# Two tuned transformer blocks on one core: the loop for overflowing experts stands ahead of the experts, and the second block's first norm shares its sums among three engines

## The chip, the cores and the metric

The kernel runs on one core of one Trainium2 chip. A core has a matrix engine (PE, with its weight loads listed apart as PEld), a vector engine (DVE), an engine for functions and scaled copies (ACT), a general engine (POOL), a queue engine that issues most transfers (SP), and 16 DMA engines that move data between the device memory and the on-chip memory. Each of the five engines runs its own list of instructions in order and waits on semaphores for the others. The metric is the device time of the core in microseconds (us).

## The reference, cut to what matters

512 tokens of width 1024 pass through two blocks, all in float32. The first ends in a mixture of 32 experts, of which each token uses two; the second begins with a norm.

```python
def hier_moe(h, w_rg, b_rg, w_re, b_re, w_gate, w_up, w_down):
    ...                                     # group and expert logits
    top_val, top_idx = lax.top_k(e_in, TOP_K)
    gate = p_grp * jax.nn.softmax(top_val, axis=-1)
    ...                                     # tokens sorted by expert
    y = (jax.nn.silu(xb @ w_gate[e]) * (xb @ w_up[e])) @ w_down[e]
    return y * wt[:, None]
    ...
# first_block
    xl = xl + gt1 * (mix_l @ w_out[l])
    h2l = modulate(rms_norm(xl, g_ffn_norm[l]), sh2, sc2)
    xl = xl + gt2 * hier_moe(...)
    return rms_norm(xl, g_final)
# second_block, one layer
    h = rms_norm_2(x, pre_w)
    proj = h @ w_in
    ...                                     # delta rule, attention, gates
    y = merged @ w_out
    return x + rms_norm_2(y, post_w)
```

Two norms follow each other directly: `rms_norm` with `g_final` ends the first block and `rms_norm_2` begins the second. The kernel folds them into one factor per token, for which it needs two sums over the 1024 columns: of x squared, and of (x times g) squared.

## The kernel before

**Stages.** `front` computes the first block up to the attention; `second` adds the out-projection, the norm and the router (`route`); `phase_moe` runs the 32 experts in 16 pairs; `tail` is the second block.

**Experts.** An expert takes at most 64 tokens in one round (`s.cap`). For a pair, a one-hot matrix `P` is built on DVE from the ranks that the router gave, `ptk` and `pgt` (four small matmuls each) read token numbers and gates out of it, POOL gathers the 128 rows of the normed tokens by an indirect DMA into `xs`, DVE or ACT scales them to `xn`, PE transposes them (`px`, copied to `xT`), and then come the products with the weights: `pgu` (gate and up, 64 matmuls a pair) and `py` (down, 32). `po` scatters the result back with a one-hot matmul and DVE adds it to `x1`. The weights of a pair are 12 tiles `we` of 1 MB. They pass through a ring of 18 buffers (`RING`), filled by SP in order; a tile is issued when the pair that used its buffer is done with it. `gather` and `gates` of the first two pairs are issued in `route` already.

**Further rounds.** If an expert has more than 64 tokens, the kernel needs further rounds: `nrounds` is computed in `route`, and a loop with a dynamic count (`tc.For_i(0, n, 1)`) behind the experts runs all 16 pairs again for the remaining tokens. With these inputs no expert has more than 64 tokens, and the count is zero. The loop's body is 3820 instructions long over all engines. Before the loop every engine reads `nrounds` into a register and branches over the body, and behind it every engine waits for the counts of all other engines and of all DMA queues before it goes on.

**The order of the work.** Around these stages a `Recorder` takes the place of the engines: it records operations, plans an order with its own costs (`plan`), picks an engine where several can do the work (`copy`, `combine`), and issues all of it at `flush` (line 1105 in nearly all rows of the profile is that one issue). There are six flushes: two in `front`, one for `second`, one for the experts, two in `tail`. A table `ORDERS` has a line for each flush: the number of operations, four parameters, and a list of shifts of priorities (`moves`). Where the number of operations isn't the one in the table, the shifts are left out (line 1090). In the kernel before, the flushes have 1160, 901, 277, 2085, 2092 and 1883 operations against 1160, 901, 306, 1107, 2092 and 1883 in the table. At the end of a flush `Recorder.before` keeps until when the engines are busy, for the next plan; line 1405, behind the loop, sets it to nothing.

**The second block's first norm.** `tail_x2` has four tiles of 128 tokens (`t`). For each, ACT squares `x1` into a scratch half and sums (`ss0`), DVE multiplies the squares by `gf2` (the square of `g_final`, one product of 128x1024) and sums (`ss1`), small DVE operations put the sums together, POOL takes the power -1/2 (`rr1`), PE transposes the broadcast factor (`pr`), and ACT copies it into `R`. Two scratch halves serve four tiles. `R` and the transposed `x1` (`pxt`) are multiplied on DVE to `xtn`, which is split into two parts (`bh`, `bl`) for the matmuls `pgm` that follow. `w2h` and `w2l` are the same split of the second block's first weights, placed at the same time.

Of the kernel before, what the change touches and what calls it, by code (L numbers as in the profile page):

```python
# [6 lines left out]
F32 = mybir.dt.float32  # L7
F32R = mybir.dt.float32r
I32 = mybir.dt.int32
AF = mybir.ActivationFunctionType  # L10
OP = mybir.AluOpType
AX = mybir.AxisListType
PSUM = bass.MemoryType.PSUM
EPS = 1e-6
# [1117 lines left out]
class Norm2:  # L1132
# [46 lines left out]
    def route(self):  # L1179


        s, rp, ps = self.s, self.rp, self.ps
        nc, V = s.nc, s.nc.vector
        T = lambda n, *sh, d=F32: rp.tile([128, *sh], d, name=n)
        wide = lambda x, n: x.unsqueeze(2).to_broadcast([128, 4, n])

        def place(v, n, name):

            eq, gt, r = T("eq" + name, 4, n, n), T("gt" + name, 4, n, n), T("r" + name, 4, n)
            one, other = v.unsqueeze(3).to_broadcast([128, 4, n, n]), v.unsqueeze(2).to_broadcast([128, 4, n, n])  # L1190
            V.tensor_tensor(eq, other, one, op=OP.is_equal)
            V.tensor_tensor(gt, other, one, op=OP.is_gt)
            V.tensor_tensor(eq, eq, self.below[:, 0:n, 0:n].unsqueeze(1).to_broadcast([128, 4, n, n]), op=OP.mult)
            V.tensor_tensor(eq, eq, gt, op=OP.add)
            V.tensor_reduce(r, eq, axis=AX.X, op=OP.add)
            return r

        gl, el = self.lg[:, :, 0:4], self.lg[:, :, 4:36]
        gm, og, ge = T("gm", 4), T("og", 4, 4), T("ge", 4, 4)
        xe, ei, two, A = T("xe", 4, 4, 8), T("ei", 4, 8), T("two", 4, 8), T("A", 4, 32, d=F32R)  # L1200
        rg = place(gl, 4, "g")
        V.scalar_tensor_tensor(xe, rg.unsqueeze(3).to_broadcast([128, 4, 4, 8]), 0.0, el.rearrange("p t (g e) -> p t g e", g=4),
                               OP.is_equal, OP.mult)
        V.tensor_reduce(ei, xe.rearrange("p t g e -> p t e g"), axis=AX.X, op=OP.add)
        V.tensor_scalar(og, rg, 0.0, None, OP.is_equal)
        og = og.unsqueeze(3).to_broadcast([128, 4, 4, 8])
        grouped = lambda x: x.rearrange("p t (g e) -> p t g e", g=4)
        spread = lambda x: x.unsqueeze(2).to_broadcast([128, 4, 4, 8])
        r = place(ei, 8, "e")
        V.tensor_scalar(two, r, 2.0, None, OP.is_lt)  # L1210
        V.tensor_tensor(grouped(A), spread(two), og, op=OP.mult)
        flat = lambda x: x.rearrange("p t e -> p (t e)")
        p = ps.tile([128, 512], F32, tag="b", name="pr")
        nc.tensor.matmul(p[:, 0:128], s.umat, flat(A), start=True, stop=False)
        for n in (3, 2, 1):
            nc.tensor.matmul(p[:, 128 - 32 * n:128], s.onesr, flat(A[:, 0:n]), start=False, stop=n == 1)
        V.scalar_tensor_tensor(flat(s.rank), p[:, 0:128], 1.0, F(flat(A)), OP.add, OP.mult)
        s.got = {e0: gather(s, e0, s.rank, s.gx, ps) for e0 in (0, 2)}
        pc = ps.tile([128, 512], F32, tag="b", name="pc")
        for n in range(4):  # L1220
            nc.tensor.matmul(pc[:, 0:32], s.onesr, A[:, n], start=n == 0, stop=n == 3)
        mx, th = T("mx", 1), T("th", 512 // s.cap)
        V.tensor_reduce(mx, pc[:, 0:32], axis=AX.X, op=OP.max)
        V.tensor_scalar(th, s.iota[:, 1:1 + 512 // s.cap], float(s.cap), None, OP.mult)
        V.tensor_scalar(th, th, mx, None, OP.is_lt)
        V.tensor_reduce(mx, th, axis=AX.X, op=OP.add)
        V.tensor_copy(s.nrounds, mx)
        ex, sm, pg, v1, v2 = (T(n, 4) for n in ("ex", "sm", "pg", "v1", "v2"))
        g1, g2, gs = T("g1", 4, 8), T("g2", 4, 8), T("gs", 4, 32)
        V.tensor_reduce(gm, gl, axis=AX.X, op=OP.max)  # L1230
        V.tensor_tensor(ge, gl, wide(gm, 4), op=OP.subtract)
        nc.scalar.activation(ge, ge, AF.Exp)
        V.tensor_reduce(pg, ge, axis=AX.X, op=OP.add)
        V.reciprocal(pg, pg)
        V.tensor_reduce(v1, ei, axis=AX.X, op=OP.max)
        V.scalar_tensor_tensor(g2, r, 1.0, ei, OP.is_equal, OP.mult)
        V.tensor_reduce(v2, g2, axis=AX.X, op=OP.add)
        V.tensor_tensor(ex, v2, v1, op=OP.subtract)
        nc.scalar.activation(ex, ex, AF.Exp)
        V.tensor_scalar(sm, ex, 1.0, None, OP.add)  # L1240
        V.reciprocal(sm, sm)
        V.tensor_tensor(sm, sm, pg, op=OP.mult)
        V.tensor_tensor(ex, ex, sm, op=OP.mult)
        V.scalar_tensor_tensor(g1, r, 0.0, wide(sm, 8), OP.is_equal, OP.mult)
        V.scalar_tensor_tensor(g2, r, 1.0, wide(ex, 8), OP.is_equal, OP.mult)
        V.tensor_tensor(g1, g1, g2, op=OP.add)
        V.tensor_tensor(grouped(gs), spread(g1), og, op=OP.mult)
        V.tensor_copy(s.gg[:, :, :, 0], gs)
        V.tensor_tensor(s.gg[:, :, :, 1], gs, F(s.gg[:, :, :, 0]), op=OP.subtract)
        for e0 in (0, 2):  # L1250
            s.got[e0] += gates(s, e0, s.got[e0][0], s.gx, ps)


def gather(s, e0, rank, pool, ps, bufs=2):
# [108 lines left out]
def phase_moe(s, last):  # L1363
    tc, nc, i = s.tc, s.nc, s.i
    right = "right"

    def load(e0):
        return s.pre.pop(e0) if e0 in s.pre else prefetch(s, e0, ahead=False)

    with ExitStack() as st:  # L1370
        s.ringD = st.enter_context(tc.tile_pool(name="ringD", bufs=RING - 17, reuse_waits="tile"))
        xp = st.enter_context(tc.tile_pool(name="xm", bufs=2, side=right, reuse_waits="tile"))
        ps = st.enter_context(tc.tile_pool(name="ps_m", bufs=8, space=PSUM, reuse_waits="tile"))
        s.nc = Recorder(nc, tc)
        for x in s.ring:
            s.nc.tile(x)
        for e0 in range(0, 32, 2):
            got = s.got.pop(e0, None)
            if got is None:
                got = gather(s, e0, s.rank, s.gx, ps)  # L1380
                got += gates(s, e0, got[0], s.gx, ps)
            moe_pair(s, e0, got, xp, ps, load)
        last()
        s.nc.flush()
        s.nc = nc

    with ExitStack() as st:
        xp = st.enter_context(tc.tile_pool(name="xg", bufs=1, side=right, reuse_waits="tile"))
        ps = st.enter_context(tc.tile_pool(name="ps_g", bufs=8, space=PSUM, reuse_waits="tile"))
        wl = xp.tile([128, 512], F32, name="wl")  # L1390
        rk = xp.tile([128, 4, 32], F32, name="rk")
        nc.vector.tensor_copy(rk, s.rank)
        n = nc.values_load(s.nrounds[0:1, 0:1], min_val=0, max_val=512)
        with tc.For_i(0, n, 1):
            nc.vector.tensor_scalar(rk, rk, -float(s.cap), None, OP.add)
            for e0 in range(0, 32, 2):
                def load1(e0):
                    def ws(m, k, a):

                        nc.sync.dma_start(wl, expert_views(s, e0 + a)[m][:, k])  # L1400
                        return wl
                    return ws
                got = gather(s, e0, rk, xp, ps, 1)
                moe_pair(s, e0, got + gates(s, e0, got[0], xp, ps), xp, ps, load1, paired=False)
    Recorder.before = ({}, {})


RING = 18
# [110 lines left out]
def tail_x2(s, ps, sp, junk, room):  # L1519
# [13 lines left out]
    V.tensor_tensor(s.col2[:, 57:65], s.col2[:, 57:65], s.col2[:, 48:56], op=OP.mult)  # L1533
    s0, s1 = (sp.tile([128, 4], F32, name=n) for n in ("ss0", "ss1"))
    r0, r1 = (sp.tile([128, 4], F32, name=n) for n in ("rr0", "rr1"))
    R = room[:, 0:512]
    nc.combine(s.gf2, s.gf, s.gf, OP.mult)
    p = ps.tile([128, 512], F32, tag="b", name="pr2")
    for t in range(4):

        sq = junk[:, 1024 * (t % 2):1024 * (t % 2) + 1024]
        a, b, r = s0[:, t:t + 1], s1[:, t:t + 1], r1[:, t:t + 1]
        nc.scalar.activation(sq, s.x1[:, t], AF.Square, accum_out=a)
        V.scalar_tensor_tensor(sq, sq, 1.0, s.gf2, OP.mult, OP.mult, accum_out=b)
        V.tensor_scalar(a, a, 1.0 / 1024, EPS, OP.mult, OP.add)
        V.tensor_scalar(r, a, EPS, None, OP.mult)
        V.scalar_tensor_tensor(r, b, 1.0 / 1024, r, OP.mult, OP.add)
        nc.gpsimd.tensor_tensor(r, r, s.mhalf[:, 0:1], op=OP.pow)
        nc.tensor.transpose(p[:, 128 * t:128 * t + 128], r.to_broadcast([128, 128]), s.ident)
        copy(nc, R[:, 128 * t:128 * t + 128], p[:, 128 * t:128 * t + 128])  # L1550
    nc.gpsimd.tensor_tensor(r0, s0, s.mhalf[:, 0:4], op=OP.pow)
    for k in range(8):
        p = ps.tile([128, 512], F32, tag="b", name="pxt")
# [580 lines left out]
```

## Time and profile before

| | us |
|---|---|
| three runs | 1357.6, 1359.11, 1359.73 (median 1359.11) |
| profiled execution | 1358.54 |
| its span, first to last instruction | 1356.8 |
| around the span | 1.7 |
| PE busy | 1270.9 (94%) |
| DVE busy | 835.1 (62%) |
| ACT busy | 483.6 (36%) |
| POOL busy | 119.0 (9%) |
| moved by DMA | 301.72 MB |
| mean granted clock of PE, share of full | 0.977 |

The times below are microseconds from the start of the span. The router ends at about 327, the experts run from there to 837, the second block from 837 to the end. "Busy" of PE is modelled from pipelined matmuls, and a busy PE can still be waiting for weights. In the views, `[x <-Y]` behind an instruction is the idle time of its engine before it and what seems to have ended it. A releaser is inferred, and where an instruction waits for nothing in the code the name given there is only what happened to end last.

### The profile page before, as it was taken

How to read it: one execution, taken by the hardware profiler on the slowest of the kernel's cores; microseconds unless marked ns; L12 is line 12 of the kernel's file. 1: busy time of each engine (PE TensorE's matmuls, PEld its weight loads, DVE VectorE, ACT ScalarE, POOL GpSimd, SP SyncE). 2: the span in 40 equal slices, each digit the busy share in tenths (PEclk: the TensorE clock that was granted, in tenths of full speed). 3: DMA queues.
4: the chain of work that ended last, by engine and by line, in shares of the span. 5: the costliest groups of instructions: out<-in, count | busy, mean ns of one | idle time of the engine just before them, and what ended most of it. 6: DMA issues, size and time to landing. Idle time of an engine off the chain costs nothing. (4 is left out here: it accounts for less than half of the span.)

```text
span 1356.8 us, 18378 instructions
## 1 busy us (share of the span) xinstructions
PE 1270.9 (94%) x7123; PEld 824.1 (61%) x7123; DVE 835.1 (62%) x1649; ACT 483.6 (36%) x992; POOL 119.0 (9%) x121
## 2 busy tenths in 40 slices
PE   5999998998999999998999996799999999999998
PEld 3778676777445444343434433578777777777786
DVE  5788899857235444444344435778544886567774
ACT  5655375312223112111110101367553775346521
POOL 1223320011000000000000001201000100000010
PEclk9999999998999999999999998799999999999999
DMA  9975320159899999999999981322111221322231
GB/s 342 325 268 178 129 79 14 49 225 413 347 420 420 420 417 419 419 420 420 419 420 419 420 316 31 124 74 83 50 47 64 63 63 63 93 63 70 99 127 62
DMA packets 94229, 301.72 MB, mean 222 GB/s; under 512 B 9915, under 2 KB 43812, under 8 KB 69558
## 3 DMA queue, kind: packets, MB, share of 16 engines
q1 hardware_dynamic: 90166, 287.87, 55.1%
q0 software_dynamic: 3392, 10.50, 2.1%
q10 hardware_dynamic: 576, 2.10, 0.4%
q8 instruction: 58, 0.95, 0.3%
q14 instruction: 37, 0.30, 0.1%
HBM read 294.14 MB, written 6.31 MB: 221 GB/s over the span
## 5 line engine op out<-in xcount | busy, mean ns | idle before, releaser
L1105 PE MATMUL pgu<-we,xT 128*64 128x512 f32 x1024 | 272.0, 600 | 0.0
L1105 PEld LDWEIGHTS pgu<-we,xT 128*64 128x64 f32 x1024 | 88.1, 138 | 138.7 <-issue 130.6
L1105 DVE TENSOR_TENSOR x<-x,po 128x512 f32<-128x512 f32 x152 | 97.2, 682 | 73.8 <-PE po L1105 73.6
L1105 PE MATMUL py<-we,hT 128*64 128x512 f32 x512 | 137.3, 604 | 3.9 <-DVE hT L1105 2.8
L1105 PE MATMUL pgm<-bl,w2h 128*128 128x512 f32 x352 | 136.2, 406 | 0.0
L1105 PE MATMUL pgm<-bh,w2h 128*128 128x512 f32 x352 | 135.7, 405 | 0.0
L1105 PE MATMUL pgm<-bh,w2l 128*128 128x512 f32 x352 | 134.7, 405 | 0.4 <-DVE w2l L1105 0.4
L1105 ACT ACTIVATE hs<-pgu 128x512 f32<-128x512 f32 x16 | 9.6, 598 | 339.3 <-PE pgu L1105 339.3
L1105 DVE SCALAR_TENSOR_TENSOR yt<-py,gs,gt 128x512 f32<-128x512 f32 x32 | 24.0, 751 | 131.4 <-PE py L1105 121.1
L1105 PEld LDWEIGHTS py<-we,hT 128*64 128x64 f32 x512 | 47.5, 138 | 66.0 <-issue 58.6
L1105 PEld LDWEIGHTS pgm<-bh,w2l 128*128 128x128 f32 x352 | 66.0, 189 | 15.2 <-issue 1.2
L1105 PEld LDWEIGHTS pgm<-bl,w2h 128*128 128x128 f32 x352 | 66.3, 189 | 14.3 <-issue 1.4
L1105 PEld LDWEIGHTS pgm<-bh,w2h 128*128 128x128 f32 x352 | 66.3, 189 | 13.8 <-issue 0.3
L1105 DVE TENSOR_TENSOR w2l<-w,w2h 128x2048 fp32r<-128x2048 f32 (+1 forms) x26 | 54.2, 2086 | 5.6 <-ACT w2h L1105 5.1
L1105 PE MATMUL po<-yh,PT 128*128 128x512 f32 x128 | 44.0, 434 | 13.2 <-DVE yh L1105 13.0
L1105 POOL DMA_INDIRECT xs<-xnd,idx x16 | 17.0, 1062 | 396.8 <-DVE idx L1105 149.6
L1105 ACT ACTIVATE xT<-px,mod 128x128 f32<-128x128 f32 x74 | 27.9, 458 | 63.4 <-PE px L1105 54.3
L1105 PEld LDWEIGHTS po<-yh,PT 128*128 128x128 f32 x128 | 23.3, 192 | 38.4 <-issue 15.1
L1105 DVE TENSOR_TENSOR hs<-hs,pgu 128x512 f32<-128x512 f32 x16 | 10.9, 684 | 56.1 <-ACT hs L1105 56.1
L1105 PE MATMUL po<-yl,PT 128*128 128x512 f32 x128 | 43.0, 424 | 2.2 <-DVE yl L1105 2.2
L1105 ACT ACTIVATE ada<-ada,sc 128x256 f32<-128x256 f32 x69 | 29.8, 501 | 17.0 <-DMA ada<-in_w_ada_dram 17.0
L1105 PEld LDWEIGHTS po<-yl,PT 128*128 128x128 f32 x128 | 24.1, 195 | 16.4 <-DVE yl L1105 6.8
(568 smaller groups left out, 2624.8 us busy)
## 6 DMA issues: line engine op xcount, KB each, us to landing
we<-in_w_gate_dram SPq DMA_DIRECT2D x64, 1024.0 KB
we<-in_w_up_dram SPq DMA_DIRECT2D x64, 1024.0 KB
we<-in_w_down_dram SPq DMA_DIRECT2D x64, 1024.0 KB
ada<-in_w_ada_dram SPq DMA_DIRECT2D x24, 1024.0 KB
w<-in_w_in_dram SPq DMA_DIRECT2D x24, 1024.0 KB
win<-in_w_in_dram SPq DMA_DIRECT2D x8, 1024.0 KB
wout<-in_w_out_dram SPq DMA_DIRECT2D x4, 1024.0 KB
wo<-in_w_out_dram SPq DMA_DIRECT2D x4, 1024.0 KB
```

What stands on the lines that cost most here:

```text
L1105: x = op.alts[e][0](*op.args, **op.kw)
```

## The change

The loop for further rounds moves from behind the experts to ahead of them, between the router and the experts, and is wrapped in a condition `tc.If(n > 0, ...)` whose false side falls through. The reset of `Recorder.before` behind the loop goes. The gather and the gates of the second pair leave `route` and are recorded with the experts, behind the loop. With this, the loop's wait for all engines and queues behind the body isn't passed when the count is zero; what an engine runs then is the reading of `nrounds`, the branch, a wait for its own count (SP: for all its transfers to have landed; POOL: for all of its own), and a branch over the body.

In `tail_x2`, the sum of (x times g) squared is made in two ways: for the first two token tiles POOL multiplies `x1` by `g_final` and ACT squares and sums; for the other two DVE does it as before. The four factors go into one tile `pr`, copied once. A few small operations are joined. The first flush of the second block has 2088 operations instead of 2092, `second` has 262 instead of 277, the experts 2100 instead of 2085; the other flushes keep their numbers.

```diff
@@ route
-        s.got = {e0: gather(s, e0, s.rank, s.gx, ps) for e0 in (0, 2)}
+        s.got = {0: gather(s, 0, s.rank, s.gx, ps)}
...
-        for e0 in (0, 2):
-            s.got[e0] += gates(s, e0, s.got[e0][0], s.gx, ps)
+        s.got[0] += gates(s, 0, s.got[0][0], s.gx, ps)
@@ phase_moe
+    with ExitStack() as st:
...
+        nc.vector.tensor_copy(rk, s.rank)
+        n = nc.values_load(s.nrounds[0:1, 0:1], min_val=0, max_val=512)
+        with tc.If(n > 0, preferred_fallthrough_block=False), tc.For_i(0, n, 1):
+            nc.vector.tensor_scalar(rk, rk, -float(s.cap), None, OP.add)
...
     with ExitStack() as st:
         s.ringD = st.enter_context(tc.tile_pool(name="ringD", bufs=RING - 17, reuse_waits="tile"))
...
-        n = nc.values_load(s.nrounds[0:1, 0:1], min_val=0, max_val=512)
-        with tc.For_i(0, n, 1):
...
-    Recorder.before = ({}, {})
@@ tail_x2
-    R = room[:, 0:512]
+    half = lambda x, n: x[:, 1024 * n:1024 * n + 1024]
+    pr = ps.tile([128, 512], F32, tag="b", name="pr2")
+    R = s.nat[1].rearrange("p c h d -> p (c h d)")[:, 0:512]
     nc.combine(s.gf2, s.gf, s.gf, OP.mult)
-    p = ps.tile([128, 512], F32, tag="b", name="pr2")
     for t in range(4):
-        sq = junk[:, 1024 * (t % 2):1024 * (t % 2) + 1024]
         a, b, r = s0[:, t:t + 1], s1[:, t:t + 1], r1[:, t:t + 1]
+        sq = half(junk, t % 2)
         nc.scalar.activation(sq, s.x1[:, t], AF.Square, accum_out=a)
-        V.scalar_tensor_tensor(sq, sq, 1.0, s.gf2, OP.mult, OP.mult, accum_out=b)
-        V.tensor_scalar(a, a, 1.0 / 1024, EPS, OP.mult, OP.add)
-        V.tensor_scalar(r, a, EPS, None, OP.mult)
+        if t < 2:
+            xg = half(room, t)
+            nc.gpsimd.tensor_tensor(xg, s.x1[:, t], s.gf, op=OP.mult)
+            nc.scalar.activation(xg, xg, AF.Square, accum_out=b)
+        else:
+            V.scalar_tensor_tensor(sq, sq, 1.0, s.gf2, OP.mult, OP.mult, accum_out=b)
+        V.tensor_scalar(r, a, EPS / 1024, EPS * EPS, OP.mult, OP.add)
         V.scalar_tensor_tensor(r, b, 1.0 / 1024, r, OP.mult, OP.add)
         nc.gpsimd.tensor_tensor(r, r, s.mhalf[:, 0:1], op=OP.pow)
-        nc.tensor.transpose(p[:, 128 * t:128 * t + 128], r.to_broadcast([128, 128]), s.ident)
-        copy(nc, R[:, 128 * t:128 * t + 128], p[:, 128 * t:128 * t + 128])
+        nc.tensor.transpose(pr[:, 128 * t:128 * t + 128], r.to_broadcast([128, 128]), s.ident)
+    copy(nc, R, pr)
+    V.tensor_scalar(s0, s0, 1.0 / 1024, EPS, OP.mult, OP.add)
     nc.gpsimd.tensor_tensor(r0, s0, s.mhalf[:, 0:4], op=OP.pow)
```

PE between the router and the first expert product, before. `warm` are matmuls whose result nobody reads:

```order
1067 L1105 MATMUL pgt<-gg,P 128x4 x8
1068 L1105 MATMUL ptk<-tokid,P 128x4 x4
1069 L1105 MATMUL pgt<-gg,P 128x4
1070 L1105 MATMUL ptk<-tokid,P 128x4 x4
1071 L1105 MATMUL pgt<-gg,P 128x4 x7
1072 L1105 MATMUL ptk<-tokid,P 128x4 x8
1073 L1105 MATMUL pgt<-gg,P 128x4 x4
1074 L1105 MATMUL px<-ident,xn 128x128 x8
1075 L1105 MATMUL pgu<-we_00_2699,xT 64x512
```

The same on PE with the change; the rows left out in the middle are the loop's body:

```order
1065 L1105 MATMUL pgt<-gg,P 128x4 x4
1066 L1376 TENSOR_LOAD nrounds
1067 L1377 COMPARE_AND_BRANCH
1068 L1377 UNCONDITIONAL_BRANCH
...
1443 L1105 MATMUL ptk<-tokid,P 128x4 x8
1444 L1105 MATMUL pgt<-gg,P 128x4 x8
1445 L1105 MATMUL ptk<-tokid,P 128x4 x8
1446 L1105 MATMUL pgt<-gg,P 128x4 x8
1447 L1105 MATMUL ptk<-tokid,P 128x4 x4
1448 L1105 MATMUL px<-ident,xn 128x128 x8
1449 L1105 MATMUL pgu<-we_00_2699,xT 64x512
```

The branch now stands between the first pair's `pgt` and everything else, and nine groups of four small matmuls stand between it and `px`.

SP at the same place, before. `we` are expert tiles, `gt_1479` the row of gates for the add:

```order
86 L1105 DMA we_04_2713<-in_w_gate_dram 128x2048
87 L1105 DMA gt_1479<-rowd 128x1024
88 L1105 DMA we_10_3121<-in_w_up_dram 128x2048
89 L1105 DMA we_10_3122<-in_w_up_dram 128x2048
90 L1105 DMA we_04_3120<-in_w_gate_dram 128x2048
91 L1105 DMA we_14_3123<-in_w_up_dram 128x2048
```

The same on SP with the change:

```order
87 L1105 DMA gt_1479<-rowd 128x1024
88 L1376 TENSOR_LOAD nrounds
89 L1376 ISA x2
90 L1105 DMA we_10_6407<-in_w_up_dram 128x2048
91 L1377 COMPARE_AND_BRANCH
92 L1377 UNCONDITIONAL_BRANCH
...
147 L1105 DMA we_10_6408<-in_w_up_dram 128x2048
148 L1105 DMA we_04_6406<-in_w_gate_dram 128x2048
149 L1105 DMA we_14_6409<-in_w_up_dram 128x2048
```

Two of the tiles that fill the ring before the experts start now stand behind SP's branch, and at that branch SP waits for everything that it has issued to land.

POOL at the second block's first norm, before (`ogT` holds `g_final`, `rr_9249` the factors of the four token tiles, `nat` the halves that take the products):

```order
56 L1105 TENSOR_TENSOR w2l<-w_2560_0_3778,w2h 128x512
57 L1105 TENSOR_TENSOR w2l<-w_2560_4_3779,w2h 128x512 x2
58 L1105 TENSOR_TENSOR rr_9249<-rr_9249,mhalf 128x1 x2
59 L1105 TENSOR_TENSOR w2l<-w_2560_0_3778,w2h 128x512
60 L1105 TENSOR_TENSOR wabl<-sv,wabh 128x64
61 L1105 TENSOR_TENSOR rr_9248<-ss_9246,mhalf 128x4
62 L1105 TENSOR_TENSOR rr_9249<-rr_9249,mhalf 128x1 x2
```

And with the change:

```order
60 L1105 TENSOR_TENSOR ogT<-ogT 128x1024
61 L1105 TENSOR_TENSOR w2l<-w_2560_0_7064,w2h 128x512
62 L1105 TENSOR_TENSOR nat_9238<-x_1468,ogT 128x1024 x2
63 L1105 TENSOR_TENSOR rr_9250<-rr_9250,mhalf 128x1 x3
64 L1105 TENSOR_TENSOR wabl<-sv,wabh 128x64
65 L1105 TENSOR_TENSOR rr_9250<-rr_9250,mhalf 128x1
66 L1105 TENSOR_TENSOR rr_9249<-ss_9247,mhalf 128x4
```

POOL takes over the product `gf2` and two products of 128x1024 and gives up three of its four `w2l`.

## Rows read from the trace of the kernel before

**Rows 1.** The page: busy time, share of the span and instructions of each engine.

```profile
PE 1270.9 (94%) x7123; PEld 824.1 (61%) x7123; DVE 835.1 (62%) x1649; ACT 483.6 (36%) x992; POOL 119.0 (9%) x121
```

**Rows 2.** Busy time in stretches; the last three columns are PE's clock, DMA share, GB/s.

```profile
328.00:340.00 12.00, 7.21 (x32) 6.98 (x33) 6.67 (x23) 0.00 (x0) 0.57 (x1) 0.50 1.01 416
340.00:344.00 4.00, 4.00 (x14) 1.79 (x14) 2.59 (x6) 1.51 (x4) 1.35 (x2) 0.50 0.79 294
344.00:348.00 4.00, 4.00 (x18) 1.48 (x16) 0.00 (x0) 0.00 (x0) 0.07 (x1) 0.90 0.48 134
348.00:352.00 4.00, 4.00 (x21) 1.66 (x19) 0.00 (x0) 0.00 (x0) 0.00 (x0) 1.00 0.86 311
356.00:800.00 444.00, 422.60 (x1880) 187.35 (x1878) 198.41 (x376) 67.92 (x126) 12.84 (x12) 0.99 1.01 419
816.00:828.00 12.00, 10.09 (x38) 3.47 (x36) 1.72 (x2) 0.00 (x0) 0.00 (x0) 0.86 0.00 0
```

**Rows 3.** Timeline from the router to the experts: start, us, instruction [idle before, releaser].

```profile
323.19 0.43 SPq L1105 DMA_DIRECT2D we<-in_w_gate_dram  x1
...
325.01 1.17 POOL L1105 DMA_INDIRECT xs<-xnd,idx  x1 [10.48 <-DVE g L1105]
...
326.08 1.02 PE L1105 MATMUL pgt<-gg,P 128*128 128x4 f32 x8
...
333.50 0.99 PE L1105 MATMUL ptk<-tokid,P 128*128 128x4 f32 x4 [0.16 <-DVE P L1105]
...
337.28 0.16 DVE L1105 CAST idx<-ptk 128x1 int32<-128x1 f32 x1 [3.24 <-DMA xs<-xnd,idx]
...
338.02 1.14 DVE L783 TENSOR_SCALAR xn<-xs,rn 128x1024 f32<-128x1024 f32 x1
...
339.22 1.97 PE L1105 MATMUL px<-ident,xn 128*128 128x128 f32 x8 [3.88 <-DVE xn L783]
...
341.12 4.16 PE L1105 MATMUL pgu<-we,xT 128*64 128x512 f32 x10
...
347.45 0.80 SPq L1105 DMA_DIRECT2D we<-in_w_up_dram  x2
```

**Rows 4.** The 16 gathers `xs` of the experts, from issue to landing.

```profile
DMA to landing us min/median/max: 4.7/9.0/12.4
```

**Rows 5.** Timeline across the loop behind the experts.

```profile
832.75 3.75 DVE L1105 TENSOR_TENSOR x<-x,po 128x512 f32<-128x512 f32 x6
...
836.55 0.42 DVE L1105 CAST w2h<-w 128x512 fp32r<-128x512 f32 x1
...
837.36 1.06 ACT L1105 ACTIVATE qT<-x 128x1024 f32<-128x1024 f32 x1 [5.67 <-DVEq L1394]
837.43 1.27 POOL L1105 TENSOR_TENSOR w2l<-w,w2h 128x512 fp32r<-128x512 f32 x1 [109.08 <-DVEq L1394]
...
839.69 4.82 PE L1105 MATMUL pxt<-ident,x 128*128 128x128 f32 x27 [5.39 <-DMA sv<-in_a_log_dram]
...
841.33 1.39 DVE L1105 CAST w2h<-w 128x512 fp32r<-128x512 f32 x1 [4.36 <-DMA caus<-in_k_mask_dram]
```

**Rows 6.** Timeline of the second block's first norm.

```profile
846.38 1.21 DVE L1105 TENSOR_TENSOR ogT<-ogT 128x1024 f32<-128x1024 f32 x1
...
847.65 1.21 DVE L1105 SCALAR_TENSOR_TENSOR qT<-qT,ogT 128x1024 f32<-128x1024 f32 x1
...
848.90 1.06 ACT L1105 ACTIVATE qT<-x 128x1024 f32<-128x1024 f32 x1 [7.15 <-DVE qT L1105]
...
850.16 2.28 POOL L1105 TENSOR_TENSOR rr<-rr,mhalf 128x1 f32<-128x1 f32 x2 [4.92 <-DVE col L1105]
...
852.42 1.94 POOL L1105 TENSOR_TENSOR w2l<-w,w2h 128x512 fp32r<-128x512 f32 x1
...
858.03 0.27 ACT L1105 COPY nat<-pr 128x128 f32<-128x128 f32 x1 [0.56 <-PE pr L1105]
858.33 1.41 DVE L1105 SCALAR_TENSOR_TENSOR xtn<-pxt,col,nat 128x512 f32<-128x512 f32 x2 [3.89 <-ACT nat L1105]
```

**Rows 7.** The second block's first flush: busy time of the stretch, columns as in rows 2.

```profile
862.00:1075.00 213.00, 211.91 (x2186) 165.44 (x2186) 138.71 (x282) 121.46 (x285) 14.00 (x16) 1.00 0.21 70
```

**Rows 8.** Who waited for whom in that stretch: total us, times, longest.

```profile
PEld pY L1105 <- issue: 4.2, 12, 0.4
...
PEld pZ L1105 <- issue: 3.8, 11, 0.4
```

More of the change, by code (lines that the diff above doesn't have):

```diff
@@ L1370, in phase_moe, with load1, ws @@
     with ExitStack() as st:
+        xp = st.enter_context(tc.tile_pool(name="xg", bufs=1, side=right, reuse_waits="tile"))
+        ps = st.enter_context(tc.tile_pool(name="ps_g", bufs=8, space=PSUM, reuse_waits="tile"))
+        wl = xp.tile([128, 512], F32, name="wl")
+        rk = xp.tile([128, 4, 32], F32, name="rk")
+        nc.vector.tensor_copy(rk, s.rank)
+        n = nc.values_load(s.nrounds[0:1, 0:1], min_val=0, max_val=512)
+        with tc.If(n > 0, preferred_fallthrough_block=False), tc.For_i(0, n, 1):
+            nc.vector.tensor_scalar(rk, rk, -float(s.cap), None, OP.add)
+            for e0 in range(0, 32, 2):
+                def load1(e0):
+                    def ws(m, k, a):
+                        nc.sync.dma_start(wl, expert_views(s, e0 + a)[m][:, k])
+                        return wl
+                    return ws
+                got = gather(s, e0, rk, xp, ps, 1)
+                moe_pair(s, e0, got + gates(s, e0, got[0], xp, ps), xp, ps, load1, paired=False)
+    with ExitStack() as st:
         s.ringD = st.enter_context(tc.tile_pool(name="ringD", bufs=RING - 17, reuse_waits="tile"))
@@ L1385, in phase_moe @@
         s.nc = nc
[L1387 to L1392, printed above, removed]
-        n = nc.values_load(s.nrounds[0:1, 0:1], min_val=0, max_val=512)
-        with tc.For_i(0, n, 1):
[L1395 to L1404, printed above, removed]
-    Recorder.before = ({}, {})
 RING = 18
```

## The prediction

> **What bounds the kernel now.** I read the page first: PE is busy 94% of the span [rows 1], so the kernel looks bound by PE. The table of stretches says that this is not one limit. From 356 to 800 the DMA share is 1.01 at 419 GB/s [rows 2]: the experts are bound by their weights, and PE's high busy share there is a model's overlap. Whatever delays the stream of weights before that stretch is paid in full behind it, since no later part of the stream has room to catch up. From 862 to 1075 PE is busy 211.91 of 213.00 us [rows 7]: the second block is bound by PE. The two seams between these stages are where nothing is full. From 816 to 828 no transfer runs [rows 2], and from 834.30 to the first `xtn` at 858.33 PE has only transposes [rows 5, 6]. [...] The change takes work from the second seam and puts some into the first. I read both in the timeline, and in the order which instructions go where.
>
> **The seam behind the experts.** The last add to `x1` ends at 832.75+3.75 = 836.50 [rows 5]. ACT and POOL, which had branched long before, go on at 837.36 and 837.43. DVE and PE had to finish first: DVE's cast ends at 836.97 and its next one, which waits for nothing in the code, starts 4.36 us later at 841.33; PE ends at 834.30 and its next starts 5.39 us later [rows 5]. So reading the count and branching over 3820 instructions costs the engine that comes last 4.4 to 5.4 us, when the DMA engines are idle. With the change this is gone here: the norm begins at 836.5, PE's transposes run right behind `po`, and the plan of the second block starts from the engines' state at the experts' end.
>
> Then the chain of the norm. Before: the squares of the third tile wait until 848.90 for a scratch half, 7.15 us, because DVE makes `gf2` at 846.38 and the first weighted sum at 847.65 only [rows 6]; then powers, two groups of transposes with four copies, and `xtn` at 858.33. After, from 836.5: ACT has six squares of 1.06 instead of four, none waiting for a half to be freed by DVE. POOL makes `gf2` before the end of the experts, then two products of 128x1024. The trace shows no such product on POOL; its 128x512 product took 1.27 us [rows 5] and 1.94 beside DVE [rows 6], so twice that, 2.5 to 3.9 us each. I take 2.5, because DVE has fewer weighted sums to run beside it: 836.5+5.1 = 841.6. The second square ends at 842.7, small operations 0.4, two powers at 1.14 each (2.28 for two [rows 6]) 845.4. Transposes and the copy: one copy in place of four, between 0.27 (one of before) and 1.08 (four), say 0.6; with 0.5 for the last transpose 846.5. DVE meanwhile has two weighted sums and seven splits of `w2`, some 9 us in all, which is the other leg and ends near 848 to 849. I take `xtn` at 849.0 against 858.33: a gain of 9.3 us. Bounds: 6, if each POOL product takes 3.9; 11, if DVE's leg is no longer than POOL's. The branch is 4.4 of it, the chain the rest.
>
> [...]
>
> **The seam ahead of the experts.** PE ends the first pair's `pgt`, half of the eight that took 1.02 [rows 3], by 327.1 at the latest and branches. I call J the time from there to its next matmul. Nine groups of four `ptk` or `pgt` follow in the new order, each about 0.99 at half clock [rows 3]: 8.9 us, with DVE's `P`, casts and reductions between. Before, seven groups (28 matmuls) stood in the same place, and DVE waited 3.24 us for a gather anyway, until 337.28 [rows 3]; this wait goes, since the second gather now stands behind the branch. Then `xn` (1.14, started 1.20 before `px`) and 1.90 from `px` to `pgu` [rows 3]. The first `pgu` comes at 327.1+J+8.9+1.2+1.9 = 339.1+J, against 341.12. J is not shown at this place. From below it is 0, if the branch is hidden as it was for ACT: `pgu` 2.0 earlier. The branch behind the experts gives 5.4: 3.4 later. [...] I take J = 6.5, nearest to the row of the same branch with a little for the load: `pgu` at 345.6, 4.5 us later.
>
> [...]
>
> SP waits at its branch until all it issued has landed, and two tiles that were issued by 323.6 [rows 3] stand behind. With 2 MB less queued the stream runs dry 5 us before 340, at 335; SP goes on 4.4 to 5.4 later, at 340, and sends 2 MB, 5 us. The stream was to pause for the ring anyway: after these two tiles all depends on the first `pgu` again, 6.33 us before the next issue [rows 3]. So SP's hole lies inside the ring's and costs nothing by itself, and the stream restarts as much later as `pgu` does. As the stretch to 800 is full, the 4.5 us arrive at its end.
>
> **The lost shifts.** The second block's first flush had its 26 shifts of priorities, since 2092 operations stood in the table; with 2088 it has none. The PE work is the same. Its chain of small products `pY` and `pZ` waits 4.2 and 3.8 us now [rows 8]. If the unshifted order covered them half as well, +8; an order without shifts may also be as good, or better by a part of the 1.1 us that PE idles, -1. As the order still has large `pgm` and `psv` between these products, I take +2. The other flushes keep their tables' state, and the first two of them their order.
>
> **Sum.** Against the profiled execution, 1358.54 (0.57 under the median of the runs, 1359.11): 1358.54 - 9.3 + 4.5 + 2 = 1355.7. It takes about 0.2%, 2.7 us, to tell a difference from none here: 1356.4 to 1361.8 is "the same".
>
> **The rivals.**
> *The branch is hidden.* J = 0, `pgu` 2.0 earlier: 1358.54 - 9.3 - 2.0 + 2 = 1349.2. For it speaks ACT, which branched early and resumed at once; against it DVE and PE, which waited 4.4 and 5.4 with nothing to wait for. Chance 0.14.
> *The branch is dear in the loaded stretch; slower than before.* The place is between `pgt` and the next `ptk` on PE. [...] It decides from J = 9.4, where the sum is 1358.5. [...] Chance 0.25.
> *The unshifted order costs what it can.* +8 in place of +2: 1361.7. For it: a long serial chain; against: 1.1 us of idle PE in 213. Chance 0.15.
> *The shared norm does nothing.* If POOL's products at 3.9 and its powers form a chain as long as DVE's was, only the branch's 4.4 remains of the gain: 1360.6, the same as before. Chance 0.10.
>
> **How the numbers follow.** My forecast, 0.36, holds 1352 to 1360 by J from 5 to 8, a gain of 8 to 11 and 0 to 4 for the order; two thirds of it lie under 1356.4. With the first rival and the good ends of the others, faster has 0.44. The rest of the forecast, the fourth rival and half of the third are the same: 0.27. Slower is the dear branch and what it adds to the third: 0.29. The range reaches from the hidden branch to two fetches, 1347 to 1367.
>
> **What would show it.** Right: behind the experts no pause of 4 us on DVE and PE, `xtn` 12 to 13 us behind the last add to `x1` instead of 22, the first `pgu` near 345.6, the time at which the DMA share falls at the end of the experts moved by the same 4 to 5, and the stretch from the first `pgm` to the end of the first flush longer by at most 4. Wrong: PE's pause behind the first `pgt` under 2 or over 9 us; an end of the experts that doesn't follow the first `pgu`; a POOL product of 128x1024 over 4 us on the way to `xtn`; new idle PE before `pY` and `pZ`.

## The result and the profile after

The changed kernel takes 1373.47 us in the median of four runs (1372.02 to 1374.86), before 1358.45: it is 1.06% slower, ratio 1.0106 with a 95% interval of 1.0092 to 1.0120. The forecast was 1355.7, with 1347 to 1367 as the range. The profiled execution took 1372.02, its span 1369.9.

The page's first part answers to [rows 1]; PE has the same 7123 instructions and is busy 7.9 us longer:

```profile
PE 1278.8 (93%) x7123; PEld 830.3 (61%) x7123; DVE 835.0 (61%) x1649; ACT 487.4 (36%) x988; POOL 120.2 (9%) x121
```

I cut both spans at the same events and subtract. Each time is the start of a row of the timelines; the last column is what the prediction had.

| stretch | before | after | change | predicted | 
|---|---|---|---|---|
| start to the first `pgu` | 341.12 | 345.72 | +4.6 | +4.5 |
| first `pgu` to the last pair's `hp` | 475.6 | 479.0 | +3.5 | 0 |
| last `hp` to the end of the last add to `x1` | 19.8 | 22.6 | +2.8 | 0 |
| last add to the first `xtn` | 21.8 | 12.1 | -9.7 | -9.3 |
| first `xtn` to the first `z` | 212.8 | 224.7 | +11.9 | +2 |
| first `z` to the end | 285.7 | 285.7 | 0 | 0 |
| span | 1356.8 | 1369.9 | +13.1 | -2.8 |

(`hp` is the product of the two halves of a pair on DVE, once a pair; the first `z` is the first score of the second block's attention, behind the first flush.) Two terms came out as predicted. Two that I had at nothing cost 6.3 us, and one that I had at 2 cost 11.9.

One trace stands behind each column, and single traces scatter. Four kernels have the orders of before up to the end of the experts (before itself and, below, the runs without shifts, with the norm alone and without the loop): in their traces the last add ends between 831.3 and 837.4, and the stretch from the first `pgu` to the last `hp` takes 473.5 to 476.7. A difference of 3 us in a stretch of the experts is therefore hardly clear of the scatter, and the two middle rows need the experiments.

**The router and the experts' start**, timeline of the kernel after, columns as in [rows 3]:

```profile
326.03 0.58 PE L1105 MATMUL pgt<-gg,P 128*128 128x4 f32 x4
326.28 16.22 SPq L1105 DMA_DIRECT2D we<-in_w_up_dram  x2
...
333.18 1.83 PE L1105 MATMUL ptk<-tokid,P 128*128 128x4 f32 x8 [6.58 <-issue]
...
342.56 1.14 DVE L783 TENSOR_SCALAR xn<-xs,rn 128x1024 f32<-128x1024 f32 x1 [0.22 <-issue]
...
343.85 1.94 PE L1105 MATMUL px<-ident,xn 128*128 128x128 f32 x8 [1.70 <-DVE xn L783]
...
345.72 15.83 PE L1105 MATMUL pgu<-we,xT 128*64 128x512 f32 x64
352.08 0.80 SPq L1105 DMA_DIRECT2D we<-in_w_up_dram  x2
```

PE stops for 6.58 us at the branch. SP's first tile behind its branch is the second of the merged 326.28 row. The next ring-limited issue is at 352.08, 6.36 behind `pgu`, as it was 6.33 behind before. At the other end of the stream the DMA share (second last column) falls some 4 to 5 us later, as the prediction had it; before, then after:

```profile
798.00:802.00 4.00, 3.77 (x17) 1.36 (x18) 2.33 (x4) 0.62 (x1) 0.00 (x0) 1.00 0.68 281
```

```profile
798.00:802.00 4.00, 4.00 (x22) 1.59 (x18) 0.00 (x0) 0.00 (x0) 0.00 (x0) 1.00 1.01 420
802.00:806.00 4.00, 3.49 (x15) 1.18 (x11) 1.39 (x3) 0.00 (x0) 0.00 (x0) 1.00 0.81 336
```

**The 13th pair.** DVE's `hp` of the 12th and 13th pair, each with PE's last large group of `pgu` of the 13th pair; first before, then after with two more rows of what lies between:

```profile
693.72 1.05 DVE L1105 TENSOR_TENSOR hp<-hs,pgu 128x512 f32<-128x512 f32 x1
...
721.04 3.65 PE L1105 MATMUL pgu<-we,xT 128*64 128x512 f32 x14
...
724.73 1.05 DVE L1105 TENSOR_TENSOR hp<-hs,pgu 128x512 f32<-128x512 f32 x1 [1.53 <-PE pgu L1105]
```

```profile
699.17 1.05 DVE L1105 TENSOR_TENSOR hp<-hs,pgu 128x512 f32<-128x512 f32 x1
...
729.21 1.14 DVE L783 TENSOR_SCALAR xn<-xs,rn 128x1024 f32<-128x1024 f32 x1
730.41 0.66 PE L1105 MATMUL px<-ident,xn 128*128 128x128 f32 x4 [1.72 <-DVE xn L783]
730.99 3.65 PE L1105 MATMUL pgu<-we,xT 128*64 128x512 f32 x14
...
734.68 1.05 DVE L1105 TENSOR_TENSOR hp<-hs,pgu 128x512 f32<-128x512 f32 x1 [4.10 <-PE pgu L1105]
```

31.0 us between them before, 35.5 after. In the new order PE makes the transposes `px` of later pairs ahead of this pair's last `pgu`, and waits for their `xn`. The pairs behind it take 30 to 31 us in both kernels, so most of the step stays. As the stream of weights falls off only 4 to 5 us later, this part of the delay isn't the stream's.

**The seam behind the experts.** Before, the last `yh` and `yl` on DVE:

```profile
828.89 0.43 DVE L1105 CAST yh<-yt 128x512 fp32r<-128x512 f32 x1
829.35 0.69 DVE L1105 TENSOR_TENSOR yl<-yt,yh 128x512 fp32r<-128x512 f32 x1
```

After, the same and the norm behind it, answering to [rows 5, 6]:

```profile
836.57 1.89 POOL L1105 TENSOR_TENSOR ogT<-ogT 128x1024 f32<-128x1024 f32 x1 [131.23 <-DMA sv<-in_w_in_dram]
...
836.93 1.82 DVE L1105 CAST yh<-yt 128x512 fp32r<-128x512 f32 x1
...
838.78 1.65 DVE L1105 TENSOR_TENSOR yl<-yt,yh 128x512 fp32r<-128x512 f32 x1
...
844.88 2.48 DVE L1105 TENSOR_TENSOR x<-x,po 128x512 f32<-128x512 f32 x4 [0.68 <-PE po L1105]
...
845.72 5.16 POOL L1105 TENSOR_TENSOR nat<-x,ogT 128x1024 f32<-128x1024 f32 x2 [5.84 <-DVE x L1105]
...
848.64 2.26 DVE L1105 TENSOR_TENSOR col<-col 128x8 f32<-128x8 f32 x1
...
858.87 0.59 ACT L1105 COPY nat<-pr 128x512 f32<-128x512 f32 x1 [5.16 <-PE pr L1105]
859.49 1.41 DVE L1105 SCALAR_TENSOR_TENSOR xtn<-pxt,col,nat 128x512 f32<-128x512 f32 x2 [2.09 <-ACT nat L1105]
```

The pauses of 4.36 and 5.39 us of [rows 5] are gone. But POOL now makes `gf2`, and a `w2l` right behind it, while DVE is in the last pair's results, and DVE's cast takes 1.82 us instead of 0.43, `yl` 1.65 instead of 0.69. From the start of the `yt` ahead of this cast to the end of the last add it is 11.2 us, 8.4 before.

**The second block's first flush**, `xtn` to `z`: busy time of the stretch, columns as in [rows 2]; before with one piece of it, then after with three, answering to [rows 7]:

```profile
858.00:1071.00 213.00, 211.22 (x2175) 163.49 (x2175) 139.14 (x279) 119.37 (x276) 12.92 (x15) 0.99 0.23 77
...
922.00:932.00 10.00, 10.00 (x58) 8.36 (x57) 7.64 (x18) 7.42 (x15) 0.00 (x0) 1.00 0.31 105
```

```profile
859.00:1084.00 225.00, 219.95 (x2175) 168.01 (x2175) 140.43 (x284) 118.88 (x270) 13.62 (x18) 0.96 0.21 71
...
916.00:922.00 6.00, 5.21 (x29) 3.92 (x27) 6.00 (x9) 4.75 (x10) 0.00 (x0) 1.00 0.07 6
922.00:932.00 10.00, 9.42 (x35) 7.51 (x35) 6.41 (x19) 3.65 (x9) 2.64 (x1) 0.54 0.60 206
932.00:938.00 6.00, 5.57 (x25) 4.08 (x24) 2.34 (x11) 3.05 (x9) 3.15 (x2) 0.91 0.00 0
```

The same 2175 PE instructions take 225 us instead of 213. PE idles 5.05 us (225 - 219.95) instead of 1.78. The granted clock is 0.96 in the mean instead of 0.99. As an estimate, a microsecond at a granted clock c loses 1-c of its work (before, four `ptk` take 0.50 us at a clock of 1.00, at 324.02, and 1.01 at 0.50, at 328.46); from the means that is 9.0 us lost instead of 2.1, each uncertain by 1 for the rounding. From the pieces it is less: from 922 to 938 5.1 us are lost (0.46 of 10 and 0.09 of 6) where nothing was lost before. So idle time and clock make 8 to 10 of the 12 us, and the rest stays open. From 922 to 932 the clock is 0.54: 0.72 in the first 2 us and 0.50 in the 8 behind them. What PE did before it fell:

```profile
917.74 1.05 PE L1105 MATMUL psq<-ones,sq 128*128 128x1 f32 x8
...
919.57 1.05 PE L1105 MATMUL psq<-ones,sq 128*128 128x1 f32 x8 [0.78 <-ACT sq L1105]
...
922.63 1.67 PE L1105 MATMUL psq<-ones,sq 128*128 128x1 f32 x8 [0.55 <-ACT sq L1105]
```

Groups of matmuls one column wide, close together, with waits for ACT ahead of them (0.78 and 0.55 us); the third already takes 1.67 us instead of 1.05. Before, the same groups come 4 to 5 us apart, with no wait, and `pgm` fills the time between them:

```profile
917.87 0.39 PE L1105 MATMUL pgm<-bh,w2l 128*128 128x512 f32 x1
918.09 0.95 PE L1105 MATMUL psq<-ones,sq 128*128 128x1 f32 x8
...
922.23 0.95 PE L1105 MATMUL psq<-ones,sq 128*128 128x1 f32 x8
```

Who waited for whom in the stretch after, answering to [rows 8]; in the stretch before no wait at `psq` is listed:

```profile
PEld pY L1105 <- issue: 5.5, 15, 0.7
...
PEld pZ L1105 <- issue: 4.1, 12, 0.4
...
PE psq L1105 <- ACT sq L1105: 1.3, 2, 0.8
```

### The profile page after: what moved, and what is told of

The parts are those of the page before. It is cut to its first block, busy times and chain, and to the rows that moved or that the text cites. A ratio compares the mean times of both kernels' runs of the same rounds, so it can differ in the third digit from the quotient of the medians.

```text
span 1369.9 us, 18350 instructions
## 1 busy us (share of the span) xinstructions
PE 1278.8 (93%) x7123; PEld 830.3 (61%) x7123; DVE 835.0 (61%) x1649; ACT 487.4 (36%) x988; POOL 120.2 (9%) x121
## 4 chain that ended last, share of the span: by engine, by line
PE 61%; issue 7%; DVE 5%; ACT 1%; POOL 1%; DVEq 0%; POOLq 0%; ACTq 0%
PE pgu L1105 16%; PE pgm L1105 14%; PE py L1105 12%; PE po L1105 5%; PE pbr L1105 3%; PE psv L1105 2%; PE C L1105 2%; PE pso L1105 1%; PE px L1105 1%; DVE yt L1105 1%; PE pZ L1105 1%; PE pY L1105 1%; DVE hp L1105 1%; DVE yl L1105 1%; PE ph L1105 1%
## 5 line engine op out<-in xcount | busy, mean ns | idle before, releaser
L1105 PE MATMUL pgu<-we,xT 128*64 128x512 f32 x1024 | 276.2, 604 | 0.0
L1105 PE MATMUL py<-we,hT 128*64 128x512 f32 x512 | 142.0, 604 | 4.6 <-DVE hT L1105 3.2
L1105 PE MATMUL pgm<-bh,w2h 128*128 128x512 f32 x352 | 129.5, 410 | 0.0
L1105 PE MATMUL pgm<-bl,w2h 128*128 128x512 f32 x352 | 129.1, 407 | 0.0
L1105 PE MATMUL pgm<-bh,w2l 128*128 128x512 f32 x352 | 128.7, 408 | 0.4 <-DVE w2l L1105 0.4
L1105 PEld LDWEIGHTS pgm<-bh,w2h 128*128 128x128 f32 x352 | 65.7, 191 | 13.1 <-issue 0.3
L1105 ACT CAST w2h<-w 128x2048 fp32r<-128x2048 f32 (+1 forms) x23 | 33.1, 1458 | 15.6 <-PE pgm L1105 8.2
```

What stands on the lines that cost most here:

```text
L1105: x = op.alts[e][0](*op.args, **op.kw)
```

## The experiments

Each ratio is to runs of the kernel before on the same chip in the same session (medians there 1356.95 to 1358.04). With the 1358.45 above, the medians of the kernel before differ by up to 1.5 us, so two experiments are best compared by their ratios. Three things had to be told apart: the lost shifts, the moved loop, and the shared norm.

**The shifts left out of the kernel before.**

```diff
-    (2092, 0.0, 1, 0, 400, (
+    (0, 0.0, 1, 0, 400, (
```

> The kernel before with one number of the table changed, so that the second block's first flush gets no shifts; all else as before. Theory (the lost shifts cost the 12 us that the changed kernel is slower between its first xtn and the first z): about 1358.5 + 12 = 1370 us, and a stretch of about 5 to 10 us between 900 and 940 in which PE's granted clock is at half. Rival (the flush is slow because of what stands ahead of it, the new norm and the later start; the shifts are worth 4 us at most): 1358 to 1362 us, PE's clock at full from 865 on.

Measured: 1375.85 us, ratio 1.0152 (1.0122 to 1.0182). One number of a table, with not an operation changed, costs 19 us. The stretch:

```profile
858.00:1087.00 229.00, 222.07 (x2178) 168.27 (x2178) 140.78 (x288) 118.74 (x268) 12.99 (x17) 0.97 0.20 66
```

16 us longer than before, with 6.9 us of idle PE and, as expected, a piece at half clock (0.50 from 922 to 928). The loss is larger than the 12 expected; idle and clock account for some 10 of the 16, the rest lies between matmuls that the profile counts as busy and stays open. PE waits for `sq` at `psq` here too (0.9 us in two waits, the longer 0.8), as in the changed kernel. The rival is out.

**The loop moved alone** (the norm of before, so 2092 operations and the shifts).

```diff
 def tail_x2(s, ps, sp, junk, room):
-    ... (the changed kernel's)
+    ... (before's)
```

> The changed kernel with the norm of before: only the loop is moved. 2092 operations, so the shifts are in force; PE's order from the first pab to the first z is that of before. Theory: start +4.6 us at the first pgu, the experts' end some 4 to 8 later than before, the branch behind them gone (4.4 less), the flush as long as before: 1358.5 + 4.6 + 3.5 - 4.4 = 1362 us, between 1358 and 1364. Rival (what stands ahead of the flush makes it slow): 1370 us or more.

Measured: 1358.93 us, 1.0016 (1.0005 to 1.0028). The flush takes 212.4 us, 212.8 before. So moving the loop is a small loss: first `pgu` at 345.02, experts' end 9.6 us later (846.10 against 836.50), `xtn` 2.2 earlier. POOL's collision with DVE is here too, with the norm of before, since there too the plan gives `gf2` to POOL (`combine` lets it choose):

```profile
835.31 1.89 POOL L1105 TENSOR_TENSOR ogT<-ogT 128x1024 f32<-128x1024 f32 x1 [131.46 <-DMA sv<-in_w_in_dram]
...
835.40 2.08 DVE L1105 CAST yh<-yt 128x512 fp32r<-128x512 f32 x1
...
837.52 1.65 DVE L1105 TENSOR_TENSOR yl<-yt,yh 128x512 fp32r<-128x512 f32 x1
```

From the last add to `xtn` it is 10.0 us, less than the 12.1 of the changed kernel with its shared norm. The time is in the range of the theory; the rival is out.

**The norm alone** (the loop behind the experts, 2088 operations, no shifts).

```diff
 def tail_x2(s, ps, sp, junk, room):
-    ... (before's)
+    ... (the changed kernel's)
```

> The kernel before with the changed norm alone; the loop stays behind the experts, 2088 operations, no shifts. Theory: the norm's chain is some 4 to 5 us shorter, the lost shifts cost 12: 1358.5 - 4.5 + 12 = 1366 us. Rival: 1354 to 1358 us.

Measured: 1371.89 us, 1.0115 (1.0093 to 1.0138). Later than the 1366 expected, because the shifts cost more than 12 on this side: the flush takes 232.9 us, and the clock falls a second time in it (0.79 from 980 to 1000, 0.87 from 1000 to 1020). The rival is out. In the first experiment, which lacks the shifts too, the median is 4 us longer, but the two intervals overlap, and the traces don't give this gain to the norm. The chain from the last add to `xtn` is 4.0 us shorter here (17.1 against 21.1), the flush 4.6 longer (232.9 against 228.3), and the last add ends 4.0 earlier (833.45 against 837.40), ahead of anything that the norm could change.

**The changed kernel with the shifts in force.**

```diff
     nc.gpsimd.tensor_tensor(r0, s0, s.mhalf[:, 0:4], op=OP.pow)
+    idle = sp.tile([128, 4], F32, name="idle")
+    for t in range(4):
+        V.memset(idle[:, t:t + 1], 0.0)
```

> The changed kernel with four tiny memsets of an unread tile in the norm, so that the flush has 2092 operations and the shifts hit the same operations as before; PE's order from the first pab to the first z is nearly that of before. Theory: 1373.5 - 12 = 1361.5 us. Rival (the shifts aren't it): 1371 to 1374 us.

Measured: 1362.15 us, 1.0040 (1.0028 to 1.0052), against 1.0106 without the four instructions: 0.66 of the 1.06% are back, 9 us by the ratios and 11.3 by the medians. The rival is out. The stretch takes 212.5 us from `xtn` to `z`, against 224.7; its clock is at 0.99, and the waits at `pY` and `pZ` are again 4.2 and 3.8, those of [rows 8]:

```profile
862.00:1075.00 213.00, 211.48 (x2177) 163.61 (x2178) 139.40 (x279) 119.74 (x277) 13.75 (x17) 0.99 0.24 79
```

**gf2 on ACT**, and **the second pair's gather back in the router**, each on the loop moved alone, then both.

```diff
-    nc.combine(s.gf2, s.gf, s.gf, OP.mult)
+    nc.scalar.activation(s.gf2, s.gf, AF.Square)
```

> The loop moved alone (norm of before, shifts in force), and the product gf2 made by ACT as a square instead of by POOL; no other operation changes its number. In the loop-alone run POOL makes gf2 from 835.31 to 837.20 and w2l right behind, and DVE's cast yh, which takes 0.43 us before, takes 2.08, its yl 1.65 instead of 0.69. Theory (POOL's products hold up DVE at the end of the experts): both go back to about 0.4 and 0.7, the last add to x1 comes 2 to 3 us sooner behind the last py, and the run is 2 to 3 us shorter than loop alone (1358.9): 1356 to 1357. Rival (DVE is slow there for another reason): cast and yl as in loop alone, time the same as loop alone.

Measured: 1356.26 us, 0.9984 (0.9975 to 0.9993), 0.32% under the loop alone (1.0016). The rival is out: DVE's operations are short again, and from the start of the `yt` ahead of the cast to the end of the last add it is 8.1 us:

```profile
838.14 0.43 DVE L1105 CAST yh<-yt 128x512 fp32r<-128x512 f32 x1
838.60 0.69 DVE L1105 TENSOR_TENSOR yl<-yt,yh 128x512 fp32r<-128x512 f32 x1
```

```diff
-        s.got = {0: gather(s, 0, s.rank, s.gx, ps)}
+        s.got = {e0: gather(s, e0, s.rank, s.gx, ps) for e0 in (0, 2)}
...
-        s.got[0] += gates(s, 0, s.got[0][0], s.gx, ps)
+        for e0 in (0, 2):
+            s.got[e0] += gates(s, e0, s.got[e0][0], s.gx, ps)
```

> The loop moved alone, but the gather and gates of the second pair stay in the router as before; the experts' flush has 2085 operations again and its PE order in the last pairs is that of before. Theory (the experts end late for two reasons: 4.5 us at the first pgu, and 4 us at the 13th pair, where the new order has px ahead of the pair's last pgu): first pgu at 343 to 344, the step of 35.5 us between the 12th and 13th hp back at about 31, experts' end 2 to 4 us later than before instead of 9.6 (of which 2.6 is POOL against DVE, which stays), time 1352 to 1355 us. Rival (the lag at the 13th pair comes from the later start and the stream of weights): the step stays near 35, and only the 1 to 2 us at the first pgu are gained: 1357 to 1358 us.

Measured: 1353.06 us, 0.9967 (0.9957 to 0.9978). The 13th pair is back at 31.0 us:

```profile
698.52 1.05 DVE L1105 TENSOR_TENSOR hp<-hs,pgu 128x512 f32<-128x512 f32 x1
...
729.54 1.04 DVE L1105 TENSOR_TENSOR hp<-hs,pgu 128x512 f32<-128x512 f32 x1 [1.53 <-PE pgu L1105]
```

So the late start isn't what delays it, but the order, which the planner made from 2100 operations instead of 2085. All traces bear this out: the step is 31.0 to 32.8 us in the eight kernels whose experts' flush has 2085 operations and 35.5 to 37.2 in the four that have 2100, and the stretch from the first `pgu` to the last `hp` is 473.5 to 477.1 in the eight and 478.3 to 481.4 in the four. The expected gain at the first `pgu` was a miss: it came at 346.56, not at 343 to 344. The experts end at 839.40, 2.9 us later than before, which is within the scatter of single traces.

> Both edits on the loop moved alone: gf2 on ACT, and the second pair's gather in the router. If both theories hold their gains add: 1350 to 1353 us. If neither does, 1358 to 1359 us as loop alone.

Measured: 1352.0 us, 0.9955 (0.9941 to 0.9969). The gains don't add in full: with the gather in the router the plan had moved POOL's product off DVE's way already. From the last but one `yt` to the end of the last add it took 8.2 us there, against 11.5 in loop alone, and POOL's product ran beside six adds that didn't become longer (3.75 us for six, as in [rows 5]):

```profile
835.06 2.43 POOL L1105 TENSOR_TENSOR ogT<-ogT 128x1024 f32<-128x1024 f32 x1 [13.22 <-DMA sv<-in_g_final_dram]
...
835.65 3.75 DVE L1105 TENSOR_TENSOR x<-x,po 128x512 f32<-128x512 f32 x6
```

**No loop**, with the orders of before: rounds beyond the first are left out, and nothing else.

```diff
-        with tc.For_i(0, n, 1):
-            ...
```

> The kernel before without the loop for further rounds (left out: rounds beyond the first, which these inputs don't need); the reset of the planner's state stays, so all orders are those of before. Theory (the branch behind the experts holds DVE 4.4 us and PE 5.4): 4 to 5 us under before, DVE's cast at 841.33 comes at 837, the norm's chain otherwise as before: about 1353 us. Rival (the pause hides behind transfers or the norm's other chain): within 1 us of before.

Measured: 1353.53 us, 0.9964 (0.9951 to 0.9977), some 5 us (0.36%) under before. The rival is out. PE goes on 1.03 us behind its last `po` and not 5.39, waiting for the add alone:

```profile
827.69 1.45 PE L1105 MATMUL po<-yl,PT 128*128 128x512 f32 x5
830.17 3.22 PE L1105 MATMUL pxt<-ident,x 128*128 128x128 f32 x27 [1.03 <-DVE x L1105]
```

**The shared norm where nothing else disturbs it**: the run with both edits, with the changed kernel's norm, `gf2` on ACT in it, and the four memsets. This is the changed kernel with three repairs.

> The loop ahead, the second pair's gather in the router, gf2 on ACT, the shifts in force by four tiny memsets, and now the shared norm (POOL multiplies x1 by g for two token tiles, one copy of the factors). So the shared norm is the one difference of weight to the run with both edits (1352.0 us). Theory (POOL's two products of 128x1024 take 2.5 us each and hold up DVE while they run, so that the shared norm is longer once nothing else delays the chain: 10.0 us from the last add to the first xtn in loop alone, 12.1 in the changed kernel): 2 to 3 us longer, 1354 to 1355 us. Rival (it was only gf2 on POOL that did harm; without it the shared norm is the shorter one): 1349 to 1351 us.

Measured: 1350.51 us, 0.9949 (0.9932 to 0.9965), the same within the intervals as without the shared norm. From the last add to `xtn` it is 11.4 us here (in the trace of an execution of 1353.74 us) and 11.3 there. The theory is out: no loss shows. The time lies in the rival's 1349 to 1351, but its reason, a shorter chain, doesn't show, and a gain of 0.06% (0.9949 against 0.9955) is far within the intervals. POOL takes 4.89 us for its two products, and DVE stands behind them: an operation on 128x8 elements takes 2.33 us beside them. In the run with both edits the first two of DVE's weighted sums take 2.16 and 2.21 us and the other two 1.21; in the run with `gf2` on ACT alone the one that runs beside a `w2l` of POOL (846.56, 1.28 us) takes 2.34 and the others 1.21 to 1.22.

**Both edits, and no loop anywhere** (rounds beyond the first left out).

```diff
-        with tc.If(n > 0, preferred_fallthrough_block=False), tc.For_i(0, n, 1):
-            ...
```

> The run with both edits, without the loop (left out: rounds beyond the first, not needed by these inputs): no branch anywhere, the planner's state carried on. The difference to the run with both edits (1352.0 us) is the price of the branch ahead of the experts. Theory (the branch stops PE for 6.6 us in the middle of a serial chain; 4 to 5 us of it arrive at the first pgu and all of these at the end): 1347 to 1348 us, first pgu at 340 to 341. Rival (the later start is made good while the experts wait for weights): 1350 to 1352 us.

Measured: 1347.58 us, 0.9922 (0.9908 to 0.9936), 4.5 us (0.33%) under the run with both edits. The first `pgu` comes 5.4 us earlier:

```profile
340.14 2.83 PE L1105 MATMUL pgu<-we,xT 128*64 128x512 f32 x6
```

The theory holds, and the rival is out. So the branch ahead of the experts costs 4.5 us at the end, the same as the branch behind them: moving it gained nothing by itself.

A gain of another kind shows against the run without the loop above, which still has the reset of the planner's state: there 0.9964, here 0.9922, some 6 us. From the last add to `xtn` it is 17.3 us there and 11.3 here. `gf2` on ACT differs too, but on the loop alone it changed this chain only from 10.0 to 10.6 us.

## Why the prediction was wrong

**The step that failed** is "The lost shifts": the unshifted order was taken at +2, bounded by -1 and +8. It cost 9 to 12 us in the changed kernel (9 by the ratios, 11.3 by the medians, 12.2 in the stretch of the traces) and 19 in the kernel before. The bound was made from the waits that are left in the order with shifts, 4.2 and 3.8 us at `pY` and `pZ` [rows 8]. These are what remains after the shifts have done their work; nothing in them says what the waits are without. And little of the loss is at `pY` and `pZ`, whose waits for issue grew by 1.6 us together, to 5.5 and 4.1. About half of it is at `psq`: PE waits 1.3 us there and is then granted about half the clock (0.54) for 10 us, which costs 4.6. That an order can cost clock, and not only idle time, was in no term. The three kernels without the shifts all show the fall (0.54 from 922 to 932 in the changed one, 0.50 from 922 to 928 in the kernel before without the shifts, 0.83 from 900 to 920 with the norm alone) and waits of up to 0.8 us at `psq`; in the changed one the two groups ahead of it start 1.83 us apart. In the kernel before the groups start 4 to 5 us apart, and the clock is at 1.00 from 880 to 1070. That these groups cause the fall wasn't tested by itself. With 11.9 in place of 2 alone, the forecast would have been 1365.6, and with the 6.3 us of the next two points 1371.9.

**The stream's delay "arrives at its end"**: right for the 4.6 us, as the last experiment and the end of the stream show. Wrong that nothing else happens there: the second pair's gather, moved out of the router, changed the number of operations in the experts' flush and with it an order 12 pairs later, 3.5 us in these two traces and 4.6 in the mean of all. I had followed the moved instructions at the place where they went, and not what the planner made of the rest.

**"POOL makes gf2 before the end of the experts"** was costed at nothing, hidden under the experts. It ran in the 2 us in which DVE makes the last results, and held DVE up: 2.8 us from the last `hp` to the last add. Its rows were in view, the 1.27 and 1.94 us of POOL's product [rows 5, 6], and I read them only as what DVE does to POOL. The trace shows the two together: POOL's product starts at 836.57 and ends at 838.46, and DVE's cast, begun at 836.93, ends at 838.75; this cast of 0.43 us takes 1.82 and 2.08 beside POOL and 0.43 once `gf2` is on ACT.

**Right:** J was 6.58 (6.5 taken) and the first `pgu` at 345.72 (345.6); SP's wait at its branch (12.1 us) hid in the ring's pause; the branch behind the experts was worth 4.4 (some 5 measured by leaving it out). That J came so close is partly luck: of the 6.5 only the 5.39 of the branch behind the experts was a row. That the load adds to it is shown by no run, nor is a fetch at the branch, which the top of the range counts twice; what the runs showed is a pause of 6.34 to 6.59 us of PE at this place.

**Right in number only:** `xtn` came 12.1 us behind the last add (12.5). The prediction made the gain of 9.3 from the branch's 4.4 and a shorter chain of the shared norm. The 9.7 measured are the branch and, by the comparison of the two runs without a loop, the planner's state that is no longer reset: with the reset the chain is 848.59 - 831.31 = 17.3 us, with the state carried on 11.3 there, 10.0 in loop alone and 11.3 to 11.4 in the two runs that differ by the shared norm. No run takes the reset alone out.

Of the rivals, the hidden branch (J of 0) and the dear one (J of 9.4 or more) are out. That the unshifted order costs what it can was right in the term, given 0.15 and a price too low by a third. That the shared norm does nothing was right of the norm where the loop stands ahead; its sum was not, since it left only the branch's 4.4 of the gain at that seam.

## What to carry to other kernels

Where an order was searched for one set of operations, count what a change does to that set first: here losing the shifts cost 9 to 19 us, more than the change could gain, and the waits in the profile of the searched order didn't bound it. An operation given to an idle engine isn't free if it holds up the busy one, as POOL's products held up DVE here (a cast of 0.43 us took 1.82 and 2.08); look at whose operations it will run beside. With the shifts in force, `gf2` on ACT and the gather left in the router the changed kernel runs at 0.9949 of before. What gains there is neither the branch's new place, which costs the same as the old one, nor the shared norm, whose gain no run can tell from nothing, but by the traces the planner's state, which is carried on once the loop no longer stands between the two stages.

## What the runs showed of the hardware

With the branch over the loop's body ahead of the experts PE stands still for 6.34 to 6.59 us in five kernels (6.58 in the changed one, 6.59 with the loop alone and with the gather back in the router, 6.35 with both edits, 6.34 with the shared norm added to them); behind the experts it was 5.39. The DMA engines are full at the first place (share 1.00 from 330 to 334 in the changed kernel) and nearly idle at the second (0.04 from 834 to 837 before), but that this makes the difference isn't shown: no run changes the load alone, and PE waits at both places for other work as well (1.35 us for `P` at the first in the kernel before, 1.03 for the add at the second in the kernel without a loop). Leaving the branch out gains 0.36% behind the experts (0.9964) and 0.33% ahead of them (0.9922 against 0.9955), 4.5 to 5 us.

A DVE operation on 128x8 elements takes 0.15 us before:

```profile
850.01 0.15 DVE L1105 TENSOR_TENSOR col<-col 128x8 f32<-128x8 f32 x1
```

In the changed kernel it took 2.26 and ended at 850.90, as POOL's second product of 128x1024 ended at 850.88: this small operation took longer there than the cast of 128x512 beside `gf2` (1.82). Not every DVE operation is held up: the six adds `x<-x,po`, which have one operand in PSUM (the matmul's output memory), took 3.75 us beside POOL's `gf2` (the run with the gather back in the router), 3.67 beside two of POOL's `w2l` (842.33, 2.53 us, the run with `gf2` on ACT) and 3.75 without POOL beside them [rows 5]. That the operand in PSUM makes this difference wasn't tested.
